# The norm between attention and the second feed-forward, taken by token blocks of 128, with the first four w_in tiles in two halves

## The chip, the cores and the metric

One NeuronCore of a Trainium2 chip runs the whole program in one launch. The metric is the device time of one execution in microseconds (us); the median of several executions is compared. All data is float32; matmul operands are in the float32r form (a float32 rounded to fewer mantissa bits).

## The reference, cut to what matters

A two-layer backbone over 256 latent tokens and 256 context tokens, with 1024 features. Layer 0 mixes tokens with an mLSTM, layer 1 with multi-head latent attention; each is followed by a convolutional feed-forward. The place of the change is in layer 1, which computes for the latent tokens alone:

```python
x = _layer_norm(ALPHA * x + ml[2] * yl, ln_g[i, 0], ln_b[i, 0])        # yl = attention @ w_out
f = _conv_ffn(_modulate(x, ml[3], ml[4]), ffn_w_in[i], ...)
x = _layer_norm(ALPHA * x + ml[5] * f, ln_g[i, 1], ln_b[i, 1])

def _conv_ffn(h, w_in, conv_w, conv_b, w_out):
    gate, up = jnp.split(h @ w_in, 2, axis=-1)                          # 1024 -> 2 x 2816
    return (jax.nn.silu(_dwconv(gate, conv_w, conv_b)) * up) @ w_out
```

The convolution runs over tokens with width 3, so it needs all 256 tokens of a feature.

## The kernel before

**Matmuls.** Every product of two float32 matrices is three float32r matmuls (`mm3`, L310 to L314): each operand is split into a rounded part `hi` and a rest `lo`, and hi·hi, hi·lo and lo·hi are added in PSUM. The split is made by a copy on ScalarE (`hi`) and a subtraction on VectorE (`lo`).

**Weights.** The class `Stream` brings the weights in a fixed order, in tiles of 128 x 1024 float32 (512 KB): a load on the SyncE (SP) queue into one of three raw buffers (L239), then the cast on ScalarE (L256) and the subtraction on VectorE (L257). The two parts go either to one of `NB = 3` buffers named `w`, which come free when the tile has been used, or, for tiles marked wide in `_plan`, to buffers named `wu` from a larger pool. `use` hands out the next tile and splits tiles ahead, up to `limit`; `pump` moves the limit and splits up to it.

**The order** of the instructions on each engine's queue is fixed when the program is built, from the order of the calls and the buffers; each engine works through its queue strictly in that order, with TensorE able to bring a weight load forward.

**The stretch of the change**, as `build` has it from L1527:

- `mla` is the attention, a generator over heads; each head gives scores (`s`), their exponentials (`P`), transposes (`PT`) and the product with the values (`o`), which is split into `oT`. The last head's product comes after the first projection weights.
- The residual rows (`res_load`, four loads) and the gate row (`bcast`, two loads) are issued on the GpSimd (POOL) queue after attention.
- The output projection `outmm("aout", ...)` gives `y` for two blocks of 128 tokens; block 0 in two pieces of 512 features, block 1 in pieces of 512, 256 and 256 (`acc4(True)`). It takes its eight weight tiles `aout`; the last seven (`TAIL`) are held, and block 0 is finished before block 1, piece by piece.
- `ln_rows` makes the residual sum and normalises the rows of one block after the other into `z` (gate multiply L946, residual add L947, statistics L949 to L956, scaling L975 to L978; the square root L953 is on ScalarE). `ln_T` transposes both blocks on TensorE (L1004), applies the modulation, one half on ScalarE (L1011) and one on VectorE (L1013), and splits into `h1` (L1016, L1017). `ln_x` scales `z` for the next residual and writes it to DRAM as `x3d`.
- `ffn_in` takes the 44 tiles `fin1` of `w_in` in pairs (gate, up). A tile is 24 matmuls: 8 feature blocks, three matmuls each, stationary the weights (128 x 128), moving the 256 tokens of `h1`. After a pair come the convolution (`conv`, L591 to L598), the product with `up` and a split into `act`.

In layer 0 there is already a form with halves: `ffn_pre` runs the first half of the first `NB` tiles over 256 of 512 tokens, and `ffn_in` runs their second half over the other 256.

```python
        st.limit = fi + QA
        k.outmm("aout", range(8 - TAIL["aout"], 8), o1, pl, 0, 8, 1, True)
        ...
        k.bg = [after0(pl, xr, gate, 1, 2, 1, 3, h1, [x3d[0], x3d[1]])]
        k.tick(1)
        st.pump(fi + QB)
        k.tick(1)
        st.pump(fi + QC)
        k.drain()
```

Of the kernel before, what the change touches and what calls it, by code (L numbers as in the profile page):

```python
# [10 lines left out]
AF = mybir.ActivationFunctionType  # L11
ALU = mybir.AluOpType
# [19 lines left out]
NB, NRAW, NU = 3, 3, 31  # L32

AHEAD = 8
QA, QB, QC = 2, 4, 6
# [31 lines left out]
def _plan():  # L67
    ids, order = {}, []

    def add(key, cols, wide=False):  # L70
        if key not in ids:
            ids[key] = (len(ids), cols)
        order.append((key, wide))

    for m in range(16):
        add(("up", m, 0), 1024)
    for s in range(4):
        for c in range(4):
            add(("og", s, c), 1024)
    for s in range(4):  # L80
        for c in range(8):
            add(("v", s, c), 1024)
    for c in range(2):
        add(("gates", 0, c), 1024)
    for h in range(H0):
        for j in range(4):
            for c in range(2):
                add(("qk", (h * 2 + j) if j < 2 else (8 + h * 2 + j - 2), c), 1024)
    for g in range(2):
        for k in range(16):  # L90
            add(("mout", 0, k), 1024, g == 1 and k >= 16 - WIDE["mout"])
    for p in range(NF):
        add(("fin0", p, 0), 1024)
        add(("fin0", p, 1), 1024)
    for g in range(2):
        for k in range(NF):
            if g == 1 and k == NF - TAIL["fout0"]:
                for c, n in enumerate((3, 3, 2)):
                    add(("dkv", 0, c), n * 320)
            add(("fout0", 0, k), 1024, g == 1 and k >= NF - WIDE["fout0"])  # L100
    for c in range(2):
        add(("ukn", 0, c), 1024, True)
    for c in range(2):
        add(("uv", 0, c), 1024, True)
    for c in range(4):
        add(("dq", 0, c), 768)
    for c, n in enumerate((2, 1)):
        add(("uqr", 0, c), n * 512)
    for c in range(3):
        add(("uqn", 0, c), 1024)  # L110
    for k in range(8):
        add(("aout", 0, k), 1024, k >= 8 - WIDE["aout"])
    for p in range(NF):
        add(("fin1", p, 0), 1024, p < 2)
        add(("fin1", p, 1), 1024, p < 2)
    for k in range(NF):
        add(("fout1", 0, k), 1024, k >= NF - WIDE["fout1"])
    return ids, order
# [165 lines left out]
class K:  # L284
# [711 lines left out]
    def ln_T(self, zs, A, B, dst, tail):  # L996

        nc = self.nc
        for kp in range(4):
# [19 lines left out]
                    yield  # L1019
            yield  # L1020

    def ln_x(self, ln, zs, dst):


        nc = self.nc
        g = self.bcast(self.a["ln_g"][ln:ln + 1, :], "gr")
        b = self.bcast(self.a["ln_b"][ln:ln + 1, :], "br")
        yield
        for t in range(2):
            for h in range(2):  # L1030
                c = slice(h * 512, (h + 1) * 512)
                nc.vector.tensor_tensor(zs[t][:, c], zs[t][:, c], g[h], op=ALU.mult)
                nc.vector.tensor_tensor(zs[t][:, c], zs[t][:, c], b[h], op=ALU.add)
                nc.gpsimd.dma_start(dst[t][:, c], zs[t][:, c])
                yield

    def outmm(self, key, ks, act, pss, toks, nk, nt, last=False):

        def mms(k, w, t, ps, cs):
            hi, lo = act(k)  # L1040
            ts = slice(toks + t * 128, toks + (t + 1) * 128)
            self.mm3(ps, (hi[:, ts], lo[:, ts]), (w[0][:, cs], w[1][:, cs]), k == 0, k == nk - 1)
        ks = list(ks)
        tail = ks[-TAIL[key]:] if last else []
        for k in ks[:len(ks) - len(tail)]:
            w = self.st.use((key, 0, k))
            for t in range(2):
                for ps, cs in pss[t]:
                    mms(k, w, t, ps, cs)
            self.tick(nt)  # L1050
        if tail:
            ws = [self.st.use((key, 0, k), hold=True) for k in tail]
            for t in range(2):
                for ps, cs in pss[t]:
                    for k, w in zip(tail, ws):
                        mms(k, w, t, ps, cs)
            self.st.unhold(key)
            self.tick(nt)

# [17 lines left out]
        return xs  # L1077


    def ffn_half(self, ps, w, hT, g):  # L1080
        gs = slice(g * 256, (g + 1) * 256)
        for k in range(8):
            c = slice(k * 128, (k + 1) * 128)
            hi, lo = hT(k)
            self.mm3(ps[:, gs], (w[0][:, c], w[1][:, c]), (hi[:, gs], lo[:, gs]), k == 0, k == 7)

    def ffn_pre(self, l, hT):

        r = []
        for n in range(NB):  # L1090
            w = self.st.use(("fin%d" % l, n // 2, n % 2), hold=True)
            ps = self.ps("fin")
            self.ffn_half(ps, w, hT, 0)
            r.append((w, ps))
        return r

    def ffn_in(self, l, hT, n, nt, pre=()):
        nc, st = self.nc, self.st
        cw, cb = self.smc("fcw%d" % l), self.smc("fcb%d" % l)
        key = "fin%d" % l  # L1100
        acts = []
        pre = list(pre)
        for p in range(NF):
            pss = []
            for j in range(2):
                if pre:
                    w, ps = pre.pop(0)
                    self.ffn_half(ps, w, hT, 1)
                    if not pre:
                        st.unhold()  # L1110
                else:
                    w = st.use((key, p, j))
                    ps = self.ps("fin")
                    for k in range(8):
                        c = slice(k * 128, (k + 1) * 128)
                        hi, lo = hT(k)
                        self.mm3(ps[:, :n], (w[0][:, c], w[1][:, c]), (hi, lo), k == 0, k == 7)
                pss.append(ps)
                self.tick(nt, 1)
            tmp = self.s2("fg")  # L1120
            self.conv(pss[0], [cw[:, j * NF + p:j * NF + p + 1] for j in range(3)], cb[:, p:p + 1], tmp, n)
            nc.vector.tensor_tensor(tmp[:, :n], tmp[:, :n], pss[1][:, :n], op=ALU.mult)
            a = self.u("act")
            nc.scalar.copy(a[:, 0, :n], tmp[:, :n])
            nc.vector.tensor_sub(a[:, 1, :n], tmp[:, :n], a[:, 0, :n])
            acts.append(a)
        return acts
# [114 lines left out]
        self.kn = [self.u("kn") for _ in range(H1)]  # L1242
        self.v1 = []

    def mla(self, hl):
        nc, st = self.nc, self.st
        st.limit = [x[0] for x in st.order].index(("aout", 0, 0))
        rows = self.dkv_rows(self.dkv_mm(hl, self.wd), 2)
# [3 lines left out]
        pss = [self.ps("dq0"), self.ps("dq1")]  # L1252
# [138 lines left out]
        for h in range(H1 + 1):  # L1391
            if 1 <= h < H1:
                st.pump(ao + h)
            if h >= 2:
                PTs[h - 2] = trans(h - 2, Ps.pop(h - 2))
            if h < H1:
                Ps[h] = scores(h)
            if h < 6 and h % 2 == 1:
                rotary(h // 2 + 1)
            if h < 2:  # L1400
                queries(h + 2)
            if h >= 2:
                attend(h - 2, PTs.pop(h - 2))
# [7 lines left out]
def build(tc, off, a, out):  # L1411
    es = ExitStack()
    with es:
# [51 lines left out]
        def after0(pss, xr, gate, g, ln, l, c, dst, xdst):  # L1465
            cond = 1 - g
            A, B = k.ln_mod_cols(ln, l, c, cond)
            yield from k.ln_rows(pss, xr, gate)
            zs = k.zs
            yield from k.ln_T(zs, A, B, dst, g == 1)  # L1470
            if xdst is not None:
                k.late.append(k.ln_x(ln, zs, xdst))
# [8 lines left out]
        k.outmm("mout", range(16 - TAIL["mout"], 16), hn, pl, 256, 16, 1, True)  # L1481
        k.hn = {}
        h0f = lambda i: (h0[i][:, 0], h0[i][:, 1])
        pre = k.ffn_pre(0, h0f)
        k.bg = [after0(pl, xr, gate, 1, 0, 0, 3, lambda i: (h0[i][:, 0, 256:512], h0[i][:, 1, 256:512]),
                       [x1d[2], x1d[3]])]
        k.drain()
# [36 lines left out]
        k.uv(0)  # L1524
        k.drain()
        k.take_late()
        att = k.mla(hl)  # L1527
        oT = next(att)
        hl = hlu = None
        o1 = lambda i: (oT[i // 2][:, 0, (i % 2) * 256:(i % 2 + 1) * 256],  # L1530
                        oT[i // 2][:, 1, (i % 2) * 256:(i % 2 + 1) * 256])
        xr = k.res_load(x2d, 0)
        gate = k.bcast(k.gd[1, 2][0:1, :], "gate")
        pl = k.acc4(True)
        k.outmm("aout", range(8 - TAIL["aout"]), o1, pl, 0, 8, 1)
        next(att)
        fi = [x[0] for x in order].index(("fin1", 0, 0))
        st.limit = fi + QA
        k.outmm("aout", range(8 - TAIL["aout"], 8), o1, pl, 0, 8, 1, True)
        oT = None  # L1540
        h1u = [k.u("h1") for _ in range(4)]
        h1 = lambda i: tuple(h1u[i // 2][:, n, (i % 2) * 256:(i % 2 + 1) * 256] for n in range(2))
        x3d = k.dr.tile([2, 128, D], F32, name="x3d")
        k.bg = [after0(pl, xr, gate, 1, 2, 1, 3, h1,
                       [x3d[0], x3d[1]])]
        k.tick(1)
        st.pump(fi + QB)
        k.tick(1)
        st.pump(fi + QC)
        k.drain()  # L1550
        st.limit = st.n
        k.take_late()
        acts = k.ffn_in(1, h1, 256, 1)
        k.drain()
        h1 = h1u = None
        act1 = lambda i: (acts[i][:, 0], acts[i][:, 1])
# [27 lines left out]
```

## Time and profile before

| | |
|---|---|
| three runs | 1432.98, 1434.51, 1434.58 us; median 1434.51 |
| profiled execution | 1434.82 us, span from first to last instruction 1433.0 |
| granted clock of TensorE, mean | 0.993 |
| busy: TensorE, VectorE, ScalarE, GpSimd | 98%, 68%, 45%, 7% of the span |
| DMA | 262.70 MB, mean 183 GB/s |
| output projection, first to last matmul | 1198.09 to 1225.41 |
| first and fifth w_in tile of layer 1 begin | 1234.66, 1246.76 |

A row of the trace in order of time gives start and length in us, engine, line, operation, output and inputs by the program's names, shapes (partitions x elements) and a count; in brackets the idle time of the engine before it and who ended that. PE is TensorE's matmuls, PEld its weight loads, DVE VectorE, ACT ScalarE, POOL GpSimd, SP SyncE. Matmuls are pipelined: the distance between two starts is the cost of one, its length is longer. In this section and below, times of the trace count from the first instruction.

### The profile page before, as it was taken

The numbers are of one execution on the slowest core, as the hardware profiler recorded it, in microseconds if no ns is written. First come the engines' busy times: TensorE is split into PE (matmuls) and PEld (weight loads), VectorE is DVE, ScalarE is ACT, GpSimd is POOL, SyncE is SP. The second block draws the span as 40 slices with busy tenths as digits, with TensorE's granted clock in tenths as the row PEclk, the third lists the DMA queues.
The fourth block names the chain that finished last, engine by engine and source line by source line (L and its number), as shares of the span: only waits on it lengthen the run. The fifth ranks groups of instructions, "written<-read, shape, count | busy, mean of one in ns | idle before, by whom it ended". The sixth has DMA issues, their size and how long they took to land.

```text
span 1433.0 us, 18800 instructions
## 1 busy us (share of the span) xinstructions
PE 1398.2 (98%) x7086; PEld 1176.4 (82%) x7086; DVE 979.7 (68%) x1436; ACT 641.8 (45%) x972; POOL 100.1 (7%) x185
## 2 busy tenths in 40 slices
PE   7999999999999999999999999999999999899997
PEld 3788888888878888888888888888888988899986
DVE  6796879885685676666778544444567887777755
ACT  6554231224334254454543333334364666555542
POOL 0011010003001010110001000000000001000000
PEclk9999999999999999999999999999999999999999
DMA  9475777778774745555636333335666315357863
GB/s 336 170 240 185 237 250 220 251 232 273 235 229 161 221 129 180 174 172 185 206 118 200 94 109 119 126 113 171 192 191 212 122 52 175 131 187 216 223 197 101
DMA packets 82827, 262.70 MB, mean 183 GB/s; under 512 B 11352, under 2 KB 19752, under 8 KB 82736
## 3 DMA queue, kind: packets, MB, share of 16 engines
q1 hardware_dynamic: 68304, 214.82, 47.7%
q0 software_dynamic: 14144, 46.17, 9.5%
q8 instruction: 55, 0.90, 0.3%
q10 hardware_dynamic: 288, 0.52, 0.1%
q14 instruction: 36, 0.29, 0.1%
HBM read 243.56 MB, written 17.91 MB: 182 GB/s over the span
## 4 chain that ended last, share of the span: by engine, by line
PE 64%; issue 18%; DVE 6%; DMA 6%; ACT 3%; POOL 2%; DVEq 0%; SPq 0%; POOLq 0%; ACTq 0%
PE fin L314 8%; PE fin L313 8%; PE fin L312 8%; PE y L313 5%; PE y L314 5%; PE y L312 5%; PE qk L314 4%; PE qk L312 4%; PE qk L313 4%; DMA raw<-in_ws 3%; DMA ar<-in_ada_w 2%; PE adar L402 1%; PE up L312 1%; DVE wu L257 1%; PE up L313 1%
## 5 line engine op out<-in xcount | busy, mean ns | idle before, releaser
L257 DVE TENSOR_TENSOR w<-raw,w 128x1024 fp32r<-128x1024 f32 (+2 forms) x267 | 323.9, 1213 | 240.5 <-ACT w L256 240.0
L256 ACT CAST w<-raw 128x1024 fp32r<-128x1024 f32 (+2 forms) x267 | 278.7, 1045 | 436.7 <-PE tok L314 152.3
L314 PE MATMUL fin<-h,w 128*128 128x256 f32 (+1 forms) x696 | 231.6, 333 | 0.5 <-DVE w L257 0.5
L313 PE MATMUL fin<-h,w 128*128 128x256 f32 (+1 forms) x696 | 231.8, 333 | 0.0
L312 PE MATMUL fin<-h,w 128*128 128x256 f32 (+1 forms) x696 | 231.7, 334 | 0.0
L437 DVE SCALAR_TENSOR_TENSOR acc<-ar,cond,acc 128x1024 f32<-128x1024 f32 x112 | 140.6, 1279 | 36.8 <-DMA ar<-in_ada_w 36.2
L314 PEld LDWEIGHTS fin<-h,w 128*128 128x128 f32 x696 | 132.2, 190 | 13.5 <-DVE w L257 0.9
L313 PEld LDWEIGHTS fin<-h,w 128*128 128x128 f32 x696 | 132.2, 190 | 13.0 <-DVE h L1017 0.2
L312 PEld LDWEIGHTS fin<-h,w 128*128 128x128 f32 x696 | 132.0, 190 | 13.1
L314 PE MATMUL qk<-xc,w 128*128 128x512 f32 x256 | 100.3, 392 | 2.0 <-DVE w L257 2.0
L312 PE MATMUL qk<-xc,w 128*128 128x512 f32 x256 | 101.1, 395 | 0.0
L312 PE MATMUL tok<-w,xm 128*128 128x512 f32 x256 | 100.4, 392 | 0.0
L313 PE MATMUL qk<-xc,w 128*128 128x512 f32 x256 | 99.9, 390 | 0.0
L314 PE MATMUL tok<-w,xm 128*128 128x512 f32 x256 | 99.7, 389 | 0.0
L313 PE MATMUL tok<-w,xm 128*128 128x512 f32 x256 | 99.6, 389 | 0.0
L312 PE MATMUL y<-w,act 128*128 128x512 f32 (+1 forms) x212 | 80.4, 379 | 0.0
L314 PE MATMUL y<-w,act 128*128 128x512 f32 (+1 forms) x212 | 80.1, 378 | 0.0
L313 PE MATMUL y<-w,act 128*128 128x512 f32 (+1 forms) x212 | 80.1, 378 | 0.0
L257 DVE TENSOR_TENSOR wu<-raw,wu 128x1024 fp32r<-128x1024 f32 x36 | 43.9, 1222 | 24.3 <-ACT wu L256 23.8
L314 PEld LDWEIGHTS qk<-xc,w 128*128 128x128 f32 x256 | 48.1, 188 | 13.1 <-DVE w L257 3.2
L312 PEld LDWEIGHTS tok<-w,xm 128*128 128x128 f32 x256 | 48.0, 188 | 10.3
L314 PEld LDWEIGHTS tok<-w,xm 128*128 128x128 f32 x256 | 48.1, 188 | 10.1
(354 smaller groups left out, 2755.1 us busy)
## 6 DMA issues: line engine op xcount, KB each, us to landing
raw<-in_ws SPq DMA_DIRECT2D x300, 512.0 KB, 3.9
ar<-in_ada_w SPq DMA_DIRECT2D x80, 512.0 KB, 4.5
adaw<-in_ada_w SPq DMA_DIRECT2D x32, 256.0 KB, 6.0
xcd<-cv POOLq DMA_DIRECT2D x16, 256.0 KB, 3.2
od<-o POOLq DMA_DIRECT2D x16, 256.0 KB, 4.2
vd<-v POOLq DMA_DIRECT2D x16, 256.0 KB, 4.0
xcr<-xcd POOLq DMA_DIRECT2D x16, 256.0 KB, 7.3
vr<-vd POOLq DMA_DIRECT2D x16, 256.0 KB, 4.0
```

The source lines that it names most:

```text
L256: k.nc.scalar.copy(h[:, :cols], raw[:, :cols])
L257: k.nc.vector.tensor_sub(l[:, :cols], raw[:, :cols], h[:, :cols])
L312: mm(out, w[0], x[0], start=start, stop=False)
L313: mm(out, w[0], x[1], start=False, stop=False)
L314: mm(out, w[1], x[0], start=False, stop=stop)
L402: nc.tensor.matmul(pr[0:4, :n], self.condr[:, k, :], x[:, c], start=k == 0 and x is hi, stop=k == 7 and x is lo)
L437: nc.vector.scalar_tensor_tensor(acc[j], w, s, acc[j], op0=ALU.mult, op1=ALU.add)
```

## The change

- Block 0 is normed, transposed and modulated while block 1 is still projected: `outmm` calls `each(t, i)` after each finished piece, which runs block 0's rows after its second piece, and block 0's transposes (new function `ln_T1`, one block of 128 tokens) after block 1's first piece.
- `ffn_pre` and `ffn_half` take a count of tiles and of tokens. The first four `fin1` tiles run over block 0's 128 tokens; then block 1 is transposed and modulated, and `ffn_in` runs the same tiles over block 1's 128 tokens. Each of the four tiles is held for both halves.
- In `ln_T1` block 0's modulation is all on ScalarE, block 1's alternates between ScalarE and VectorE; the splits take two feature blocks at a time.
- Of the first four tiles only the second pair is marked wide; the first pair uses the `w` buffers. The limits of the stream move accordingly.
- Residual and gate loads are issued before the scores of the seventh head (`mid`); the scaling and writing of `x3d` starts five ticks later, in `ffn_in`.

```diff
     for p in range(NF):
-        add(("fin1", p, 0), 1024, p < 2)
-        add(("fin1", p, 1), 1024, p < 2)
+        add(("fin1", p, 0), 1024, p == 1)
+        add(("fin1", p, 1), 1024, p == 1)
...
+    def ln_T1(self, z, A, B, t, hu):
+        nc = self.nc
+        for kp in range(2):
+            pt = self.ps("zT")
+            for i in range(4):
+                k = kp * 4 + i
+                nc.tensor.transpose(pt[:, i * 128:(i + 1) * 128], z[:, k * 128:(k + 1) * 128], self.ident)
+            tmp = self.s2("zm")
+            for i in range(4):
+                k = kp * 4 + i
+                c = slice(i * 128, (i + 1) * 128)
+                if i % 2 == 0 or t == 0:
+                    nc.scalar.activation(tmp[:, c], pt[:, c], AF.Identity, bias=B[:, k:k + 1], scale=A[:, k:k + 1])
+                else:
+                    nc.vector.tensor_scalar(tmp[:, c], pt[:, c], A[:, k:k + 1], B[:, k:k + 1],
+                                            op0=ALU.mult, op1=ALU.add)
+                if i % 2:
+                    src = tmp[:, (i - 1) * 128:(i + 1) * 128].rearrange("p (k c) -> p k c", k=2)
+                    hi, lo = [hu[k // 2][:, n].rearrange("p (k c) -> p k c", k=2)[:, :, t * 128:(t + 1) * 128]
+                              for n in range(2)]
+                    nc.scalar.copy(hi, src)
+                    nc.vector.tensor_sub(lo, src, hi)
...
-    def outmm(self, key, ks, act, pss, toks, nk, nt, last=False):
+    def outmm(self, key, ks, act, pss, toks, nk, nt, last=False, each=None):
...
-                for ps, cs in pss[t]:
+                for i, (ps, cs) in enumerate(pss[t]):
                     for k, w in zip(tail, ws):
                         mms(k, w, t, ps, cs)
+                    if each is not None:
+                        each(t, i)
...
-    def ffn_half(self, ps, w, hT, g):
-        gs = slice(g * 256, (g + 1) * 256)
+    def ffn_half(self, ps, w, hT, g, n=512):
+        gs = slice(g * n // 2, (g + 1) * n // 2)
...
-    def ffn_pre(self, l, hT):
+    def ffn_pre(self, l, hT, nt, n):
...
+            if h == 6:
+                mid()
...
+        xg = []
+
+        def mid():
+            xg.extend((k.res_load(x2d, 0), k.bcast(k.gd[1, 2][0:1, :], "gate")))
+
+        att = k.mla(hl, mid)
...
-        st.limit = fi + QA
-        k.outmm("aout", range(8 - TAIL["aout"], 8), o1, pl, 0, 8, 1, True)
+        st.limit = fi
...
-        k.bg = [after0(pl, xr, gate, 1, 2, 1, 3, h1,
-                       [x3d[0], x3d[1]])]
-        k.tick(1)
-        st.pump(fi + QB)
-        k.tick(1)
-        st.pump(fi + QC)
-        k.drain()
+        A, B = k.ln_mod_cols(2, 1, 3, 0)
+        rows = k.ln_rows(pl, *xg)
+
+        def each(t, i):
+            if (t, i) == (0, 1):
+                next(rows)
+                st.pump(fi + 2)
+            elif (t, i) == (1, 0):
+                k.ln_T1(k.zs[0], A, B, 0, h1u)
+                st.pump(fi + 4)
+
+        k.outmm("aout", range(8 - TAIL["aout"], 8), o1, pl, 0, 8, 1, True, each)
+        oT = None
+        next(rows)
+        pre = k.ffn_pre(1, h1, 4, 256)
+        st.pump(fi + 5)
+        k.ln_T1(k.zs[1], A, B, 1, h1u)
         st.limit = st.n
+        k.late.extend([iter(range(5)), k.ln_x(2, k.zs, [x3d[0], x3d[1]])])
         k.take_late()
-        acts = k.ffn_in(1, h1, 256, 1)
+        acts = k.ffn_in(1, h1, 256, 1, pre)
```

More of the change, by code (lines that the diff above doesn't have):

```diff
@@ L1085, in ffn_half @@
             self.mm3(ps[:, gs], (w[0][:, c], w[1][:, c]), (hi[:, gs], lo[:, gs]), k == 0, k == 7)
-    def ffn_pre(self, l, hT):
+    def ffn_pre(self, l, hT, nt, n):
         r = []
-        for n in range(NB):
-            w = self.st.use(("fin%d" % l, n // 2, n % 2), hold=True)
+        for i in range(nt):
+            w = self.st.use(("fin%d" % l, i // 2, i % 2), hold=True)
             ps = self.ps("fin")
-            self.ffn_half(ps, w, hT, 0)
+            self.ffn_half(ps, w, hT, 0, n)
             r.append((w, ps))
@@ L1107, in ffn_in @@
                     w, ps = pre.pop(0)
-                    self.ffn_half(ps, w, hT, 1)
+                    self.ffn_half(ps, w, hT, 1, n)
                     if not pre:
@@ L1243, in mla_kv, with mla @@
         self.v1 = []
-    def mla(self, hl):
+    def mla(self, hl, mid):
         nc, st = self.nc, self.st
@@ L1483, in build @@
         h0f = lambda i: (h0[i][:, 0], h0[i][:, 1])
-        pre = k.ffn_pre(0, h0f)
+        pre = k.ffn_pre(0, h0f, NB, 512)
         k.bg = [after0(pl, xr, gate, 1, 0, 0, 3, lambda i: (h0[i][:, 0, 256:512], h0[i][:, 1, 256:512]),
@@ L1526, in build @@
         k.take_late()
-        att = k.mla(hl)
+        xg = []
+        def mid():
+            xg.extend((k.res_load(x2d, 0), k.bcast(k.gd[1, 2][0:1, :], "gate")))
+        att = k.mla(hl, mid)
         oT = next(att)
@@ L1531, in build @@
                         oT[i // 2][:, 1, (i % 2) * 256:(i % 2 + 1) * 256])
-        xr = k.res_load(x2d, 0)
-        gate = k.bcast(k.gd[1, 2][0:1, :], "gate")
         pl = k.acc4(True)
@@ L1537, in build @@
         fi = [x[0] for x in order].index(("fin1", 0, 0))
-        st.limit = fi + QA
-        k.outmm("aout", range(8 - TAIL["aout"], 8), o1, pl, 0, 8, 1, True)
-        oT = None
+        st.limit = fi
         h1u = [k.u("h1") for _ in range(4)]
```

## The prediction

> **What bounds the kernel now.** I read the page's busy table first, then TensorE's rows in order of time around the join of attention and feed-forward, then the weight loads beside them, then the queues of VectorE and ScalarE in that stretch.
>
> ```profile
> PE 1398.2 (98%) x7086; PEld 1176.4 (82%) x7086; DVE 979.7 (68%) x1436; ACT 641.8 (45%) x972; POOL 100.1 (7%) x185
> ```
>
> TensorE bounds the kernel: busy for 98% of the span. A change helps if it closes one of TensorE's few gaps, and hurts if it gives TensorE more work where there is no gap. The gap this change aims at shows in TensorE's rows (start, length, operation, idle before it and who ended that):
>
> ```profile
> 1225.05 0.28 PE L312 MATMUL y<-wu,oT 128*128 128x256 f32 x1
> 1225.17 0.28 PE L313 MATMUL y<-wu,oT 128*128 128x256 f32 x1
> 1225.29 0.28 PE L314 MATMUL y<-wu,oT 128*128 128x256 f32 x1
> 1226.03 0.44 PE L1004 MATMUL zT<-ident,z 128*128 128x128 f32 x2 [0.46 <-ACT z L975]
> 1226.74 0.44 PE L1004 MATMUL zT<-ident,z 128*128 128x128 f32 x2 [0.27 <-ACT z L978]
> 1232.19 2.82 PE L1004 MATMUL zT<-ident,z 128*128 128x128 f32 x12 [5.01 <-DVE z L977]
> 1234.66 0.56 PE L312 MATMUL fin<-h,wu 128*128 128x256 f32 x1
> ```
>
> The output projection starts its last matmul at 1225.29, the feed-forward its first at 1234.66. Between lie 16 transposes and the wait for block 1's norm (5.01). The same stretch by windows, with the granted clock after the five engines' busy times:
>
> ```profile
> 1225.40:1234.66 9.26, 3.52 (x18) 2.88 (x17) 7.20 (x17) 5.78 (x10) 0.00 (x0) 0.69 0.62 201
> ```
>
> The clock falls to a mean of 0.69 here, so the last 12 transposes take 0.213 each (from 1232.19 to 1234.66 with their start), where eight others at full clock take 0.87 together, 0.109 each (L1366 in the chain of waits). After 1234.66 TensorE has no gap for over 150 us: whatever the gap gives or the new matmuls cost goes to the end undiminished. The fifth w_in tile begins at 1246.76 (first `fin<-h,w` row); all sums run to that point. Before, it lies 1246.76 - 1225.41 = 21.35 us behind the end of the projection.
>
> **The price that decides: a matmul 128 columns wide.** Each of the first four tiles is 24 matmuls of 256 tokens, one every 0.120 (1225.05, 1225.17, 1225.29 above). The change makes them 48 of 128 tokens, each with its own weight load: 192 in place of 96. No row shows a 128-wide matmul on these fp32r operands, so it is bounded. From below: steps are 0.227 for 512 columns, 0.173 for 384, 0.147 for 320, 0.120 for 256, that is 0.0135 and 0.417 ns a column; 128 columns by this line are 0.067. But every matmul also loads 128 columns of weights. Where TensorE comes out of a wait, two loads stand directly behind one another (first fence 512 wide, second 256 wide):
>
> ```profile
> 420.34 0.19 PEld L314 LDWEIGHTS qk<-xc,w 128*128 128x128 f32 x1 [2.22 <-DVE w L257]
> 420.45 0.19 PEld L312 LDWEIGHTS qk<-xc,w 128*128 128x128 f32 x1
> 420.68 0.19 PEld L313 LDWEIGHTS qk<-xc,w 128*128 128x128 f32 x1
> ```
>
> ```profile
> 1196.55 0.19 PEld L313 LDWEIGHTS o<-PT,v 128*128 128x128 f32 x1 [0.60 <-DVE PT L318]
> 1196.66 0.19 PEld L314 LDWEIGHTS o<-PT,v 128*128 128x128 f32 x1
> 1196.78 0.19 PEld L312 LDWEIGHTS o<-PT,v 128*128 128x128 f32 x1
> ```
>
> With no matmul in the way the next load comes 0.11 later; after that a load starts when the matmul ahead of it starts. Also, the second 512-wide matmul starts at 420.68, 0.34 after the first load; less its step of 0.227 that leaves 0.113 from load to stream. A load of 0.109 to 0.113 hides behind 0.120 of matmul, not behind 0.067. So I take 0.113 a half matmul, with ends 0.067 (loads wholly hidden) and 0.120 (a half costs what a whole does). A tile then takes 48 x 0.113 = 5.4 instead of 2.9.
>
> [...]
>
> **The change part by part**, on the times of before.
>
> 1. *End of attention.* In the built order ScalarE's queue now has a copy (oT, 0.37) and an exponential (P, 0.69) ahead of, and another 0.69 between, the two PT copies that the seventh head's product waits for; before, both copies stood first (that product waited 0.36 there). The end goes from 0 to 1.3 later; I take the middle, **+0.7**. The six residual and gate loads on GpSimd's queue come earlier; before they landed by 1193 and were first used at 1216, so no cost.
>
> 2. *Norm of block 0 inside the projection.* Its eight transposes now stand in TensorE's queue after 28 of the last 42 matmuls, 14 x 0.120 = 1.7 before the end, at 1223.7, and everything behind them waits. In before these transposes could start at 1226.03. ScalarE now has one weight cast less (0.95) ahead of the square root, so 1225.1. Stall **+1.4**, then 8 x 0.109 = 0.87; the projection ends at 1225.41 + 2.27 = 1227.7.
>
> 3. *First halves.* Block 0's h comes from ScalarE: 8 activations 128 wide (0.40 each at L812, about 0.34 apart) and 4 copies (0.31 apart), 4.0 us from 1226.0, and a subtraction of 0.42: the last quarter is there at 1230.4. The first tile's 19th matmul wants it at 1227.7 + 18 x 0.113 = 1229.7. Wait **0.8**. Then 96 x 0.113 = 10.85: first halves end at 1239.3.
>
> 4. *Norm of block 1.* VectorE's new order puts the subtractions of tiles 3 and 4 ahead of block 1's first gate multiply, and these wait for ScalarE's casts, which stand behind block 0's copies: casts from 1230.1 to 1232.1, second subtraction done at 1233.3. Queued behind it: the whole norm of block 1, then its transposes. That chain took 1224.39 to 1231.59 before, with two subtractions (2.3) in it: 4.9 by itself, so z at 1238.2, its halves done by 1239.0. TensorE arrives at 1239.3: the norm is just covered. If the halves were short the cover would be gone, and TensorE would stand until about 1238.7 (rivals).
>
> 5. *Second halves.* 8 transposes 0.87, to 1240.2. The next matmul needs an activation (0.43), VectorE's half of it (0.41) and a copy (0.41) on the first four, and later quarters are waited for again: **2.0** in all, from 0 if the order were ideal to 3. Then 96 x 0.113 = 10.85: the fifth tile starts at 1253.1, before 1246.76: **+6.3**.
>
> Taken from before and already in these differences: the 5.01 wait and the half clock (12 x 0.104 = 1.25 on transposes). With no TensorE wait above some 2 us I expect the clock to stay up.
>
> Edits at no cost: tile order and number of loads on SP's queue stay. Loads of tiles 6 and 7 start when the late subtractions free their buffers, near 1233 instead of 1221 to 1224, and are wanted after 1250: 4.4 to land and 2.3 to split are hidden; without that cover up to 3. Only one w buffer is left while two tiles are held; the sixth tile is split once the first tile's second half is done (2.3 plus waits, against three halves, 8.1). The final scaling of x3d moves some ticks later; it is first read for the load at 1296.87 and used by the last norm after 1424.
>
> Sum: +0.7 + 6.3 = **+7.0**. The profiled execution took 1434.82 (span 1433.0 and 1.8 around it), 0.3 over the median of 1434.51; 1434.51 + 7.0 = **1441.5**.
>
> **Rivals.**
>
> *Loads hidden, halves cheap.* For it: in steady 256-wide work the step follows columns, and loads are never seen to limit. Against it: the 0.11 between loads. At 0.067 the first halves end at 1227.7 + 0.8 + 6.4 = 1234.9, but block 1's z is there only at 1238.7 (step 4); matmuls again from 1240.4, with 0.9 of further waits and 6.4: 1247.7, +0.9, with +0.7 **1436.1**. [...]
>
> [...]
>
> *Faster.* Mechanism: block 1's norm is wholly hidden by the first halves. Place: VectorE's queue behind block 0's subtractions, if the two late casts come in time. With no waits in steps 1 and 2, the fifth tile would start at 1230.0 + 192 steps; it equals 1246.76 at 0.087 a step, and at 0.067 it is 1242.9: -3.9, **1430.6**. It decides below 0.087 only, and the loads speak for 0.11.
>
> *Several passes.* The fp32 transposes, 128 wide, take 0.109, more than 0.067: narrow moving operands may be slower. Doubled passes would still give 0.120 (my upper end, +1.3). Four would give 0.227: 192 x 0.114 = 21.9 more, **1463**. No row shows it.
>
> *No difference.* The built order shows the halves and the early norm, so the change does what it says; but the last projection waits for loads (1.2 us of TensorE idle from 1387 to 1425) and some delay could be absorbed: 1435 to 1437 if the smallest ends also hold.
>
> **How the numbers follow.** Forecast 0.74, cheap halves 0.10, faster 0.05, four passes 0.07, no difference 0.04. The forecast's own range from the open terms (step 1: 0 to 1.3; half matmul 0.109 to 0.120: -0.8 to +1.3; waits of step 5: -2 to +1; late loads up to +3) is about 1438.5 to 1446. With the cheap halves it reaches down to 1436; that leaves out some 0.13. About 0.2% (2.9 us) is what a measurement of this kernel can tell from no change: faster (below 1431.6) 0.05; same 0.12, the fourth rival and most of the first; slower 0.83.
>
> **What would show it.** Right: `fin<-h` matmuls 128 wide, 0.11 apart with a load at the start of each; TensorE's gap of 5 us gone, clock near 1.0; transposes of block 0 with about 1.4 idle ahead; the fifth tile some 27 to 28 us behind the end of what was the projection's work. Wrong: steps of 0.07 or of 0.2; a wait of several us ahead of block 1's transposes; a new idle on TensorE after the fourth tile.

## The result, and the profile after

The changed kernel takes 1447.65 us (median of 4 runs, 1446.48 to 1450.27) against 1433.74 for the kernel before; the ratio is 1.0106 (95% interval 1.0094 to 1.0118), some 15 us. The sign of the prediction was right; the time lies above its range of 1436 to 1446.

TensorE is still busy for 98% of a span that has become longer (the first row of the page's busy table):

```profile
PE 1417.2 (98%) x7182; PEld 1194.9 (83%) x7182; DVE 979.5 (68%) x1436; ACT 644.5 (45%) x980; POOL 100.0 (7%) x185
```

It gained 96 matmuls, as planned, and 19 us of busy time. TensorE's rows in order of time show where. Around the norm of block 0, the first halves, and the step from first to second halves:

```profile
1221.28 0.28 PE L312 MATMUL y<-wu,oT 128*128 128x256 f32 x1
1222.96 0.66 PE L1029 MATMUL zT<-ident,z 128*128 128x128 f32 x4 [1.40 <-ACT z L975]
...
1225.48 0.28 PE L314 MATMUL y<-wu,oT 128*128 128x256 f32 x1
1225.60 0.23 PE L312 MATMUL fin<-h,w 128*128 128x128 f32 x1
...
1236.95 0.28 PE L314 MATMUL fin<-h,wu 128*128 128x128 f32 x1
1237.06 1.06 PE L1029 MATMUL zT<-ident,z 128*128 128x128 f32 x8
1239.11 0.44 PE L312 MATMUL fin<-h,w 128*128 128x128 f32 x2 [0.99 <-ACT h L1043]
...
1242.18 0.28 PE L312 MATMUL fin<-h,w 128*128 128x128 f32 x1
1242.30 0.36 PE L313 MATMUL fin<-h,w 128*128 128x128 f32 x1
1242.46 0.42 PE L314 MATMUL fin<-h,w 128*128 128x128 f32 x1
1242.67 0.41 PE L312 MATMUL fin<-h,w 128*128 128x128 f32 x1
1242.89 0.41 PE L313 MATMUL fin<-h,w 128*128 128x128 f32 x1
```

The stall of 1.40 ahead of block 0's transposes, the steps of 0.11 and the short wait of 0.99 for block 1's h are as forecast, and there is no wait ahead of block 1's transposes: its norm was covered. Then, at 1242.3, in the middle of a row of like matmuls, the step goes from 0.11 to 0.213 and stays there. The same stretch by windows (window, its length, busy time and count of TensorE, weight loads, VectorE, ScalarE, GpSimd, then the granted clock, and last the DMA engines' busy share and GB/s):

```profile
1225.60:1237.06 11.46, 11.23 (x98) 10.90 (x97) 8.62 (x18) 5.21 (x11) 1.09 (x2) 1.00 0.49 139
1237.06:1242.34 5.28, 4.15 (x32) 3.49 (x31) 3.00 (x8) 3.07 (x9) 0.00 (x0) 1.00 0.00 0
1242.34:1258.25 15.91, 15.91 (x78) 15.91 (x76) 5.07 (x8) 5.52 (x8) 0.00 (x0) 0.50 0.23 67
1258.25:1262.82 4.57, 4.57 (x22) 4.57 (x23) 0.85 (x2) 0.40 (x1) 0.00 (x0) 0.50 0.00 0
1262.82:1277.00 14.18, 14.18 (x121) 14.18 (x120) 12.01 (x18) 8.08 (x12) 1.09 (x2) 1.00 0.55 159
```

TensorE's clock was halved for 20.48 us, from 1242.34 to 1262.82, while TensorE was busy the whole time. It is the one large thing that the prediction did not have. Its price: about 74.6 steps of 0.213 instead of 0.111 up to the fifth tile (7.6 us), and 4.57 us of whole tiles with steps of 0.213 instead of 0.120 (2.0 us): 9.6 us in all.

The account of the two traces, counted from the first score of the last heads, since the profiled runs reach that point 2.75 us apart in a part of the program that the change does not touch (in the other runs below it lies anywhere from 1154.1 to 1158.4): from there to the fifth tile 88.76 us before and 103.00 after, +14.2; behind it +1.7; together +16, of which 9.6 are the clock.

### The profile page after: what moved, and what is told of

Same layout as the page of the kernel before. It is cut to its first block, busy times and chain, and to the rows that moved or that the text cites. A ratio compares the mean times of both kernels' runs of the same rounds, so it can differ in the third digit from the quotient of the medians.

```text
span 1446.2 us, 19000 instructions
## 1 busy us (share of the span) xinstructions
PE 1417.2 (98%) x7182; PEld 1194.9 (83%) x7182; DVE 979.5 (68%) x1436; ACT 644.5 (45%) x980; POOL 100.0 (7%) x185
## 4 chain that ended last, share of the span: by engine, by line
PE 64%; issue 18%; DMA 6%; DVE 6%; ACT 3%; POOL 2%; SPq 0%; DVEq 0%; POOLq 0%; ACTq 0%
PE fin L314 9%; PE fin L313 9%; PE fin L312 9%; PE y L313 5%; PE y L314 5%; PE y L312 5%; PE qk L314 4%; PE qk L312 4%; PE qk L313 4%; DMA raw<-in_ws 3%; DMA ar<-in_ada_w 2%; DVE wu L257 1%; PE up L312 1%; DMA xcr<-xcd 1%; PE up L314 1%
## 5 line engine op out<-in xcount | busy, mean ns | idle before, releaser
L312 PE MATMUL fin<-h,w 128*128 128x256 f32 (+2 forms) x728 | 242.6, 334 | 1.1 <-ACT h L1043 1.0
L313 PE MATMUL fin<-h,w 128*128 128x256 f32 (+2 forms) x728 | 243.0, 334 | 0.3
L314 PE MATMUL fin<-h,w 128*128 128x256 f32 (+2 forms) x728 | 242.6, 334 | 0.5 <-DVE w L257 0.5
L312 PEld LDWEIGHTS fin<-h,w 128*128 128x128 f32 x728 | 140.2, 193 | 14.3 <-ACT h L1043 1.4
L314 PEld LDWEIGHTS fin<-h,w 128*128 128x128 f32 x728 | 140.6, 193 | 13.8 <-DVE w L257 0.9
L313 PEld LDWEIGHTS fin<-h,w 128*128 128x128 f32 x728 | 140.5, 193 | 13.8 <-DVE h L1044 0.9
```

What stands on the lines that cost most here:

```text
L312: mm(out, w[0], x[0], start=start, stop=False)
L313: mm(out, w[0], x[1], start=False, stop=False)
L314: mm(out, w[1], x[0], start=False, stop=stop)
```

## Experiments: what lowers the clock

**Two theories.** In the records of the granted clock all spells at half clock that end before the record does are multiples of 3.41 us long: 3.41 (e4_second_wide), 6.83 (the kernel before), 13.65 (e5_early_only), 20.48 (the changed kernel), 47.79 (e1_halves_start), 58.03 (e3_quarters_mid). Two falls of one trace also lie whole multiples apart: 16.95 and 1242.34 in the changed kernel (359.0 of them), 17.14 and 1228.88 in the kernel before (355.0). So I take it that the clock is decided on a grid of stretches of that length. *Share theory*: what counts in a stretch is the part of it in which TensorE streams columns. By the steps of 0.120 us for 256 columns and 0.227 for 512 in the trace of before, a column takes 0.417 ns at full clock; by that estimate a 128-wide matmul streams for 53 ns of its step of 111. The last stretch ahead of the fall (1238.92 to 1242.34) held 22 such matmuls, 2816 columns: a share of 0.34; the pure halves ahead of it had 0.47 to 0.48. At half clock 16 halves in a stretch are a share of 0.50; after the four stretches of it from 1242.34 on the clock did not come back. *Wait theory*: the waits between 1237.9 and 1241 lower the clock, and the width does not matter.

**The second pass made wide** (e4_second_wide). Edit, in `ffn_in` for layer 1:

```diff
-                    self.ffn_half(ps, w, hT, 1, n)
+                    self.ffn_half(ps, w, hT, 0, 2 * n)
```

> The changed kernel, but the second pass over the first four tiles takes all 256 tokens again (block 0 is computed twice, the values are the same), so that its 96 matmuls are 256 wide. Waits are as in the changed kernel. Share theory (the clock falls because TensorE streams for too small a part of the time: a 128-wide matmul streams 128 columns, 53 ns at full clock, in a step of 111 ns): the second pass streams for some 0.9 of its time, the clock stays at 1.0, the fifth tile comes 16 us or less behind the first transposes of block 1, and the time is that of the changed kernel less the 9.7 us that its 20.48 us at half clock cost, plus 96 x 0.009 = 0.9: about 1439. Wait theory (the clock falls because of the 1.0 us wait and the small waits behind it, whatever the width): the clock falls at the same place, for at least one period of 6.8 us: 1442 or more.

Measured: 1440.34 us, ratio to before 1.0058 (1.0043 to 1.0073). The window of the second pass, and the whole tiles behind it:

```profile
1242.00:1254.55 12.55, 11.61 (x97) 11.61 (x98) 7.99 (x16) 7.98 (x16) 0.00 (x0) 1.00 0.23 55
1254.55:1260.00 5.45, 5.45 (x48) 5.45 (x47) 2.14 (x4) 1.92 (x3) 0.00 (x0) 1.00 0.17 70
```

The clock stays at 1.00 with the same waits, and doing block 0 twice makes the kernel some 7 us faster. The waits alone do not do it. It is no luck of the grid either: shifting the grid over this trace from 1230.5 on, I find no stretch under 0.44. (The clock did fall earlier in this trace, from 1227.08 to 1230.49, after the stretch with the stall of 1.89 inside the projection, which had a share of 0.35; it was back just after the first halves began at 1229.95.)

**Halves and quarters where nothing waits** (e2_halves_mid, e3_quarters_mid). In the kernel before, tiles of chosen pairs are run in parts of the tokens (`PARTS` is `{(1, 6): 2, (1, 7): 2}` in the first kernel, `{(1, 6): 4, (1, 7): 2}` in the second; the keys are layer and pair):

```diff
-                    for k in range(8):
-                        ...
-                        self.mm3(ps[:, :n], (w[0][:, c], w[1][:, c]), (hi, lo), k == 0, k == 7)
+                    q = PARTS.get((l, p), 1)
+                    for g in range(q):
+                        gs = slice(g * n // q, (g + 1) * n // q)
+                        for k in range(8):
+                            ...
+                            self.mm3(ps[:, gs], (w[0][:, c], w[1][:, c]), (hi[:, gs], lo[:, gs]), k == 0, k == 7)
```

> The kernel before, with four tiles in the middle of the second feed-forward (pairs 6 and 7) each run as two halves of 128 tokens, one behind the other: 192 matmuls 128 wide where TensorE waits for nothing. It prices the half by itself. Both theories: steps of 0.111 against 0.120 for twice the width, 192 x 0.111 - 96 x 0.120 = +9.8 us, 1443.5. Share theory: 0.48 of the time streaming for 21 us; in the changed kernel two such stretches of 3.4 us did not lower the clock, so it should stay at 1.0, but only just. Wait theory: it stays at 1.0 with nothing to wait for.

Measured: 1444.67 us, ratio 1.0087 (1.0072 to 1.0102). In its trace the four tiles take 21.39 us instead of 11.52, a step of 0.111, +9.9:

```profile
1269.83:1291.22 21.39, 21.39 (x194) 21.39 (x193) 8.78 (x14) 6.98 (x11) 0.00 (x0) 1.00 0.41 121
```

So the deciding price of the prediction (0.113) holds, and 21 us of unbroken halves, at a share of 0.47 to 0.48 in every stretch, leave the clock at 1.00.

> The kernel before, with pair 6 of the second feed-forward in quarters of 64 tokens (192 matmuls 64 wide) and pair 7 in halves (96 matmuls 128 wide), no waits anywhere near. Share theory: with the load still setting the step (0.111) a quarter streams 27 ns, a share of 0.24, below the 0.34 at which the clock fell in the changed kernel; the clock falls to 0.5 within 3.4 to 10.2 us though TensorE never waits, steps double to 0.213, and it stays there through the halves of pair 7 (share 0.5 at half clock, as in the changed kernel) until whole tiles are back: about 61 x 0.111 + 131 x 0.213 + 96 x 0.213 = 55 us in place of 11.5, with 2.5 behind it some +46: 1480. Wait theory: nothing waits, the clock stays at 1.0, 288 x 0.111 - 96 x 0.120 = +20.5: 1454.

Measured: 1479.26 us, ratio 1.0334 (1.0316 to 1.0351). By windows: whole tiles, quarters, quarters, halves, whole tiles, whole tiles:

```profile
1255.00:1264.88 9.88, 9.88 (x84) 9.88 (x83) 7.20 (x11) 5.00 (x8) 0.00 (x0) 1.00 0.62 199
1264.88:1267.77 2.89, 2.89 (x29) 2.89 (x27) 2.17 (x4) 1.38 (x3) 0.00 (x0) 1.00 0.62 181
1267.77:1303.07 35.30, 35.30 (x167) 35.30 (x167) 2.53 (x4) 2.32 (x4) 0.00 (x0) 0.50 0.10 30
1303.07:1323.59 20.52, 20.52 (x98) 20.52 (x98) 4.09 (x6) 3.28 (x5) 0.00 (x0) 0.50 0.15 52
1323.59:1325.80 2.21, 2.21 (x11) 2.21 (x12) 1.31 (x2) 1.35 (x2) 0.00 (x0) 0.50 0.00 0
1325.80:1340.00 14.20, 14.20 (x121) 14.20 (x120) 8.83 (x14) 7.06 (x11) 0.00 (x0) 1.00 0.53 154
```

TensorE is busy in every microsecond of this table, and the clock falls 2.9 us after the quarters begin (share of that stretch 0.34), holds through 20.5 us of halves, and returns 2.2 us after whole tiles are back (share of that stretch 0.78). This is the decisive run: narrow matmuls alone lowered the clock, with no wait in sight. The number of matmuls or of weight loads in a stretch can't be the measure, since quarters and halves come at the same step of 0.111.

**Halves that begin at half clock** (e1_halves_start). The same edit with `{(1, 0): 2, (1, 1): 2}`: the first four tiles in halves, but after the whole norm as before.

> The kernel before, with its first four tiles each in two halves of 128 tokens, one behind the other, after the whole norm; the norm is as before, so the 5 us wait and the clock at half from about 1229 are there when the first tile begins. Share theory: if the clock is not given back in the period in which the first matmuls start, the halves (share 0.5 at half clock) can't bring it back: 192 x 0.213 = 41 us in place of 11.5 (half of the first of it at half clock already), +30 to +32: about 1465; if it is given back by the transposes and first matmuls, it stays up, 192 x 0.111 - 96 x 0.120 = +9.8: 1443.5. Wait theory: it is given back within 6.8 us of the end of the wait in any case: +9.8 to +13, 1443 to 1447.

Measured: 1462.44 us, ratio 1.0215 (1.0199 to 1.0230).

```profile
1234.06:1275.13 41.07, 41.07 (x194) 41.07 (x193) 11.45 (x24) 6.72 (x15) 2.18 (x4) 0.50 0.07 27
1275.13:1277.67 2.54, 2.54 (x13) 2.54 (x14) 0.85 (x2) 0.40 (x1) 0.00 (x0) 0.50 0.00 0
```

The clock that fell in the old 5 us wait stays at half through all 192 halves, 41 us, and returns 2.5 us into the whole tiles. In the kernel before, with whole tiles in that place, it returned after one spell of 6.83 us (1228.88 to 1235.70).

**Filling the wait with useless wide work** (e6_warm_after). To the changed kernel, behind block 1's transposes:

```diff
         k.ln_T1(k.zs[1], A, B, 1, h1u)
+        wm = k.ps("wm")
+        for i in range(8):
+            nc.tensor.matmul(wm[:, :256], pre[0][0][0][:, :128], pre[0][0][0][:, :256], start=True, stop=True)
```

> The changed kernel with eight matmuls 256 wide added behind block 1's transposes, on weights, their result unused: 8 x 0.120 = 0.96 us of more work in the place of the 0.99 us wait for block 1's h. The halves stay narrow. Share theory: the stretch of 3.4 us around the wait streams for about 0.5 of its time instead of 0.34, as the stretches ahead of it did, the clock stays at 1.0, and the time is that of the changed kernel less 9.7: 1438, although TensorE has more to do. Rival (what lowers the clock is the length of the narrow stretch, the second pass above all, and the wait has no part in it): the clock falls as before, 1447 to 1449.

Measured: two groups. Two runs took 1438.62 and 1440.19 at a mean clock of 0.996, two took 1448.64 and 1447.38 at 0.989 and 0.990; the median of 1443.78 and the ratio of 1.0076 (1.0048 to 1.0104) mix them. The profiled run is of the first group, and its second pass keeps the clock:

```profile
1238.50:1251.21 12.71, 12.54 (x106) 11.90 (x105) 7.98 (x16) 8.20 (x16) 0.00 (x0) 1.00 0.23 61
```

Half as expected: where it works, 8 more matmuls take 8 to 9 us off; but something else lowers the clock in other runs. No run of the second group was traced, so where the clock fell in it is not shown. My next guess was the stall inside the projection (in this very trace the clock fell there for 3.41 us and came back just ahead of the halves).

**The loads back in their old place** (e8_warm_after_late_loads), as the kernel just above, with `mid` called behind attention:

> As e6_warm_after, but the residual and gate loads are issued behind attention again, as in the kernel before. From the first score of the last heads to the projection's first matmul the kernels with early loads took 1.3 us more than those with late ones. If this is the order of the last heads' instructions, 1.3 comes off: 1436.7, and the stretch has its old length of 40.1. Rival (the loads themselves are the cause and the first gate multiply then waits for them): no gain, 1438.

Measured: 1440.02, 1437.14, 1436.68 at 0.996 to 0.998, and 1444.76, 1446.00 at 0.990. By time this can't tell a gain of 1.3 from none. The trace can: from the first score of the last heads to the projection's first matmul it is 40.09 us (1158.42 to 1198.51), exactly as in the kernel before and its variants, and 41.41 to 41.43 in all kernels with early loads. Issuing the loads early costs 1.3 us. With them ScalarE's order changes too: in the changed kernel an exponential (P) of 0.7 us stands ahead of each of the last four PT copies in front of the projection, and TensorE waits up to 0.96 there for PT, where the kernel before waits 0.36; with late loads the old order is back. So the cause is most likely the order, but no run changed it without the loads.

**Both waits filled** (e9_warm_both), and the changed kernel once more beside it (e10_after_again). Block 0's transposes behind the whole projection, ten wide matmuls behind them, and the eight from above:

```diff
             elif (t, i) == (1, 0):
-                k.ln_T1(k.zs[0], A, B, 0, h1u)
                 st.pump(fi + 4)
+            if (t, i) == (1, 2):
+                k.ln_T1(k.zs[0], A, B, 0, h1u)
+                wm = k.ps("wm")
+                wt = st.hl[fi][0]
+                for _ in range(10):
+                    nc.tensor.matmul(wm[:, :256], wt[:, :128], wt[:, :256], start=True, stop=True)
```

> As e6_warm_after, and the other wait ahead of the narrow matmuls is filled too: block 0's transposes stand behind the whole output projection instead of 14 matmuls ahead of its end (so that the projection does not stand 1.4 to 1.9 us for block 0's norm), and ten matmuls 256 wide on weights, result unused, follow them while block 0's h is made. Of the runs of e6_warm_after two had a mean clock of 0.996 and took 1438.6 and 1440.2 us, two had 0.989 and 0.990 and took 1448.6 and 1447.4. Share theory: in the slower two the clock fell in the wait inside the projection, and the narrow matmuls behind it could not bring it back; with that wait gone too no stretch of 3.4 us is under 0.4, all runs have 0.995 or more and lie between 1436 and 1441. Rival (halves of 0.48 lower the clock by themselves in some runs): two groups again, some runs at 0.99 and 1446 to 1449.

Measured: not as expected. Three runs at 1439.88 to 1441.20 (0.996), three at 1445.14 to 1448.41 (0.988 to 0.991). The stall was not the (only) cause. But my claim that no stretch was under 0.4 was wrong too. In the first halves three waits of 0.28 us for quarters of h remain (steps of 0.39 at 1226.19, 1227.19 and 1228.20), and the first 3.5 us look like this:

```profile
1225.32:1228.80 3.48, 3.20 (x25) 2.71 (x23) 2.33 (x6) 2.51 (x8) 0.92 (x2) 1.00 0.11 36
```

The columns in it give the 3.41 us from 1225.39 a share of 0.33. Shifting the grid over the trace, a stretch under 0.37 occurs in 43% of the positions, under 0.38 in 48%: three of six runs fit that, though none of the three was traced. In the traces that show a fall the grid lies elsewhere each time: counted from the first instruction, a boundary stands at 0.1 us in the kernel before, 3.3 in the changed kernel, 1.7 in e4_second_wide, 1.4 in e3_quarters_mid and 2.5 in e5_early_only (the time of the fall there, less whole stretches of 3.4133). So I take it that the same program can fall in one run and not in the next.

> The changed kernel unchanged, beside e9_warm_both on the same chip, to see whether it has the two groups of e6_warm_after. Share theory: its wait ahead of the second pass is always there, and the second pass is narrow, so nearly every run has a mean clock of 0.991 or less and takes 1445 to 1450. Rival (chance of the run): a part of the runs at 0.996 and 1438.

The changed kernel itself: 1447.64 to 1451.77 in five runs, all at 0.988 to 0.991, ratio 1.0113 (1.0095 to 1.0132). With the four runs of the result that is nine of nine: with its longer wait unfilled it falls nearly wherever the grid lies. Counted in the same way, with the second halves carried on at full clock behind the fall, a stretch under 0.37 occurs in 80% of the positions, under 0.38 in 93%.

**All waits filled** (e11_all_filled). 36 instead of 10 wide matmuls ahead of the first pass, 28 instead of 8 ahead of the second, so that neither pass waits inside:

> As e9_warm_both with more filling: 36 matmuls 256 wide instead of 10 behind block 0's transposes, 28 instead of 8 behind block 1's, so that both passes start only when all of h is there. This adds 26 + 20 matmuls of 0.120, 5.5 us, and takes away the small waits inside the passes: of the three of 0.28 us at 1226 to 1228 of e9_warm_both and the four of 0.1 to 0.25 at 1238 to 1241. With these waits, the stretch of 3.4 us from 1225.39 streams for 0.33 of its time, and about 0.4 of all positions of the 3.4 us grid hold a stretch under 0.37, as three of the six runs of e9_warm_both fell to half clock. Share theory: the narrow passes alone are at 0.48, as in e2_halves_mid, no stretch is under 0.45, all runs have a mean clock of 0.995 or more and lie together, about 3 to 4 us above the better group of e9_warm_both: 1443 to 1445. Rival (the narrow passes lower the clock by chance of the run, whatever the waits): two groups again, some runs at 0.99 and 1450 or more.

Measured: six of six runs at a mean clock of 0.996 to 0.998, 1439.82 to 1441.96, median 1440.89, ratio 1.0061 (1.0048 to 1.0074). The first pass, the filling and the second pass:

```profile
1227.30:1237.90 10.60, 10.60 (x98) 10.60 (x96) 4.56 (x13) 1.11 (x2) 0.55 (x1) 1.00 0.19 50
1238.00:1242.20 4.20, 4.20 (x38) 4.20 (x37) 2.88 (x8) 3.02 (x8) 0.00 (x0) 1.00 0.01 4
1242.30:1252.89 10.59, 10.59 (x98) 10.59 (x96) 5.10 (x9) 5.42 (x8) 0.00 (x0) 1.00 0.29 75
```

The lowest share over all positions of the grid is now 0.47, and the second group is gone. The time is 2 to 4 us below what I had written. From the first score to the fifth tile it is 98.7 us against 95.6 in the profiled run with less filling, the 3 us expected; behind the feed-forward that other run took 2 us more (72.3 against 70.0 from its last w_in matmul to the end), and I had built on its total.

**What the early norm and the halves are worth** (e5_early_only). The changed kernel with `ffn_pre(1, h1, 0, 256)`, no halves at all:

> The changed kernel without the first halves: block 0 is normed and transposed inside the projection as in the changed kernel, block 1 behind it, and all tiles run 256 wide. It shows what the halves are worth. TensorE stands from the projection's end to block 1's h, some 12 to 13 us, and the clock falls in that time, but comes back with the first whole tiles: the fifth tile about 24.5 us behind the projection's end, 1438 to 1441. Share theory: the halves as priced in e2 give nothing back, since each half that fills the wait costs 2.45 later; this time is within 2 us of that of e4_second_wide. Rival (the halves do hide the norm, and only the clock spoilt it): this one is slower than e4_second_wide by 4 us or more.

Measured: 1440.30 us, ratio 1.0051 (1.0034 to 1.0067), like the kernel with the wide second pass (1.0058). TensorE stands much longer than before ahead of block 1's transposes:

```profile
1235.81 1.97 PE L1029 MATMUL zT<-ident,z 128*128 128x128 f32 x8 [11.03 <-DVE z L977]
1238.62 0.58 PE L312 MATMUL fin<-h,w 128*128 128x256 f32 x1 [0.84 <-ACT h L1043]
```

The new order puts two subtractions of weights ahead of block 1's norm on VectorE and makes a 5 us wait one of 11. (The clock fell in this wait too, for 13.65 us from 1227.85 on.) The halves then fill that wait, at a price that eats the gain: from the first score to the fifth tile 96.8 us without halves, 96.7 with the wide second pass, 88.8 in the kernel before.

**Filling the wait of the kernel before** (e7_warm_before). The finding used on the kernel before: 22 wide matmuls, result unused, in its old 5 us wait.

```diff
         st.pump(fi + QB)
+        wm = k.ps("wm")
+        wt = st.hl[fi][0]
+        for i in range(22):
+            nc.tensor.matmul(wm[:, :512], wt[:, :128], wt[:, :512], start=True, stop=True)
```

> The kernel before with 22 matmuls 512 wide on weights, result unused, behind the last matmul of the output projection: 22 x 0.227 = 5.0 us of work in its 5 us wait for block 1's norm. Share theory: no stretch of 3.4 us falls below a third, the clock stays at 1.0 through the join, the 12 transposes take 1.3 instead of 2.6 and the first tile loses nothing: 1.5 to 2 us less, 1431 to 1432. Rival (the clock at the join costs nothing, or the filling delays the norm): no change, or up to 1 us more.

Measured: 1430.93 us against 1432.88, ratio 0.9988 (0.9979 to 0.9997), 1.7 us faster: a small gain, whose interval only just leaves out no change. The join, and the 12 transposes in it:

```profile
1222.80:1231.71 8.91, 7.20 (x41) 5.79 (x40) 7.23 (x16) 5.82 (x10) 0.00 (x0) 1.00 0.64 211
```

```profile
1222.85 5.18 PE L1551 MATMUL wm<-wu 128*128 128x512 f32 x22
1229.76 1.53 PE L1004 MATMUL zT<-ident,z 128*128 128x128 f32 x12 [1.29 <-DVE z L977]
```

The clock is 1.00 where it was 0.69, and the 12 transposes take 1.53 instead of 2.82. From the projection's last matmul to the fifth tile it is 20.6 us instead of 21.5 in the profiled runs; more of the 1.7 I can't place.

## Why the prediction was wrong

Point by point, from the first score of the last heads:

| step | forecast | measured |
|---|---|---|
| 128-wide matmul | 0.113 | 0.111 |
| 1. end of attention | +0.7 | +1.3 |
| 2. stall ahead of block 0's transposes | 1.4 | 1.40 (0.93 to 1.89 in other runs with this order) |
| 2. first to last matmul of the projection | +2.27 | +1.6 |
| 3. waits in the first halves | 0.8 | 11.46 - 96 x 0.111 = 0.8 |
| 4. norm of block 1 | just covered | covered: first half of z 0.3 us ahead of TensorE |
| 5. waits in the second halves | 2.0 | 21.19 - 7.6 - 0.9 - 10.66 = 2.0 |
| fifth tile without the clock | +7.0 | 14.2 - 7.6 = +6.6 |
| the clock | none | +9.6 |

**The step that failed** is the sentence behind step 5: "With no TensorE wait above some 2 us I expect the clock to stay up." I had read the fall of the clock in the trace of before as the result of a 5 us wait, and so looked only for long waits. In the runs the clock goes with how much of each 3.41 us TensorE streams: halves with no wait sit at 0.47 to 0.48 and kept it up (e2_halves_mid), and with a wait of 0.99 us and some smaller ones behind it the stretch was at 0.34, and it fell. The longest idle of the stage was 1.40 us, and with quarters the clock fell with none at all, so no bound on the length of waits could have told. The row that could have said so was in the prediction: a step of 0.113 in which the columns take 0.053 is half empty although the page counts TensorE as busy. With the clock held (second pass wide, or all waits filled) the kernel is at ratios of 1.0058 and 1.0061, 8 to 9 us above the kernel before, where 7.0 were forecast; both do extra matmuls for it. Closest to the changed kernel are the two runs of e6_warm_after that kept the clock, with 1 us of extra matmuls in a wait: 5.7 and 7.3 us above the median of the kernel before beside them (1432.88). So the rest of the sum was about right, and the miss is the clock.

Step 2 was a little too high because of a wait for a weight tile inside the projection: the step there, 1.38 us between two matmuls in the trace of before, shrank to 0.40. The sum had not allowed for that. Of the rivals, cheap halves and several passes fall with the step of 0.111, in both widths below 256: a quarter takes 0.111 too, as long as the 0.11 from one weight load to the next, so I take it that the load sets the step. The faster one falls with the same number.

## What to carry to other kernels

Splitting a matmul along its moving side below 256 columns gains no time here, since a part of 128 or of 64 columns costs 0.111 us where 256 cost 0.120, and loads of weights follow one another 0.11 apart; fill a wait with narrow matmuls only if the columns you double cost less than the wait. Work out the share of time in which columns stream, per 3.4 us, not the share in which TensorE is busy: in these traces the clock halved behind shares of 0.35 and less and stayed at 0.47, and once it was down 41 us of halves did not bring it back (e1_halves_start). A short wait can then be worth filling with wide matmuls, useless ones if need be: in the kernel before that gained 1.7 us.

## What the hardware showed that I had not expected

- TensorE's clock fell to half with TensorE busy all the time (e3_quarters_mid, 1267.77). Over all traces of this study, it fell after every stretch with a share of 0.35 or less (0.35 in e4_second_wide, 0.34 in e3_quarters_mid and in the changed kernel) and after none with 0.41 or more (0.41 in the changed kernel from 1225.27, 0.44 in the kernel before from 1088.93), as I count it from the matmuls' rows (transposes of float32 with twice their columns, as they take 0.109 for 128). The two stretches nearest to the limit lie between: 0.37 in e6_warm_after, where it fell, and 0.38 at the start of e10_after_again, where it stayed. The doubling is needed: with 128 columns a transpose, a stretch of e7_warm_before that is mostly transposes (from 1228.03) would be at 0.22, and the clock stayed up.
- It came back after every stretch of 0.78 or more (0.78 in e3_quarters_mid, 0.98 in the kernel before up to 1235.70), and after none of 0.64 or less (0.64 in the kernel before from 17.14, 0.63 in the changed kernel from 1255.99). Halves at half clock are at 0.50: through all 41 us of them in e1_halves_start and 20.5 in e3_quarters_mid it stayed down.
- At full clock 64 and 128 columns both take 0.111 (e3_quarters_mid, e2_halves_mid); at half clock 64 columns (e3_quarters_mid), 128 and 256 (the changed kernel) all take 0.213.
- The same program had two groups of times, around 1440 and 1448 (e6_warm_after, e9_warm_both), which the mean clock tells apart (0.996, and 0.988 to 0.991). My reading is that its shares are near the limit and that the grid lies elsewhere in each run, as it does in the traces.
